# An encoder block on one core: branch A's queries and keys stored by map and loaded over 128 partitions, two gate products moved into branch A's stage

## The chip, the cores and the metric

The kernel runs on one core of a Trainium2 chip. The metric is the device time of one execution in microseconds, lower is better. A core has TensorE (PE, matmuls), VectorE (DVE), ScalarE (ACT), GpSimd (POOL) and SyncE (SP). SP issues every transfer of this kernel on one queue, in order; a transfer that has to wait holds all that are behind it in the queue. Sixteen DMA engines carry the transfers. SBUF, the on-chip memory, has 128 partitions; a tile is partitions x elements.

## What is computed

One encoder layer on 1024 tokens and 16 meta tokens of width 1024 in float32. Two attention branches run in parallel from the same normed input, are merged by two sigmoid gates, and a SwiGLU block follows:

```python
proj = rms_norm(h) @ w_in
# qa, ka: 4 heads x 2 maps x 64;  va: 4 heads x 128;  qb, kb, vb: branch B;  ga, gb: 1024 each
attn = softmax(q1 k1 / 8 + bias) - lam * softmax(q2 k2 / 8 + bias)     # branch A, per head
y_a  = rms_norm(attn @ va) * (1 - lambda_init)
y_b  = windowed attention with sinks (window 128, 8 heads on 2 key heads)
merged = sigmoid(ga) * (y_a @ w_ba) + sigmoid(gb) * (y_b @ w_bb)
h = h + merged @ w_o
h = h + (silu(h' @ w_gate) * (h' @ w_up)) @ w_down                     # h' = rms_norm(h)
out = rms_norm(h)[:, N_META:]
```

## The kernel before

**Numbers as pairs.** Each float32 operand of a matmul is split into a high part (ScalarE, a rounded copy) and a low part (the difference, by VectorE or GpSimd). A product is then three matmuls: high x high, high x low, low x high. `hT_hi` and `hT_lo` hold the normed, transposed input; the function `quad(hl, kh, half)` names a quarter of one of them (four of the eight row blocks, 512 of the tokens).

**Queries and keys of branch A.** `project_a(h)` projects head h: the queries in two chunks of 512 tokens, the values, and the keys in three chunks (384, 384, 272). Each chunk is copied out of PSUM into a stage tile (tag `qk`, three buffers, `QK_BUFS`), high part beside low part, and stored to DRAM by `q_consume` (L543) or `k_consume` (L546). The 128 partitions of a stage tile are map m = 0 or 1 times 64 elements. In DRAM, `qa_d[h]` and `ka_d[h]` are laid out [high or low, 128, tokens], so one store from all 128 partitions writes a chunk.

The score matmuls want it the other way round: for one map, partitions 0 to 63 hold the high part and 64 to 127 the low part, with a second copy of the keys in which the halves are swapped (`ks[m][:, 1]`). Two matmuls, one with each copy, then sum the products of high and low parts. `load_q` (L650) brings one map's queries with two transfers of 64 partitions, `load_k` (L654) its keys with four. `load_a1(h)` loads map 1 of head h, `load_a0(h)` map 0 and the values. The tiles have one buffer, so a transfer waits until the head before has made its last scores on that tile. `load_a1(0)` and the keys of map 0 of head 0 are asked for early, among the projections.

**Gate projections.** They are computed by a scheme with seven products per block of 256 gate columns in place of eight. A product (p, k) has number p and block k = 0 to 7; it is 12 matmuls, run in four steps of three. Products 5, 6, 7 and 3 use sums of weights, made by GpSimd (`weight_sums`) and kept in `ws_d`; products 5, 6, 7 and 4 use sums of token blocks, kept in `ts_d` and loaded over a quarter of `hT` by `load_sums` (L575) once that quarter is no longer read: number 5 over quarter (0, 1), and second, number 6 over quarter (1, 0). Product 2 needs no sums of either kind and reads quarter (1, 0). Before branch A starts, a loop (L711 to L722, matmuls at L718) runs product 2 for all eight k. All others are in `order_g` (L579): first (5, k) and (3, k), then (1, k), (6, k), (7, k), (4, k). `gate_steps` (L729, matmuls at L738) is a generator that yields after each step of `order_g`, and `g_ahead` (L636) asks for the weights (`g_load`, L620) four products ahead and splits them three ahead. The weights of the first two products are loaded and split before the stage, into tiles named `w_g` and `w_gop`.

**Branch A's stage.** Four heads of eight tiles of 128 queries. A tile makes scores for map 1, then map 0 (L797, three chunks of keys, two matmuls each), exponentials, the combination, transposes (L823), and the value matmuls (L836) of earlier tiles come in between. `SLOTS` mixes in one step of the gates at four places of a tile. `fill(n)` runs n steps at once: `G_HEAD` (10) at the start of heads 1 to 3, `G_FIRST` (0) at the start of head 0, `G_LAST` (4) after the last tile; `HOLD` (26) steps are kept for the end, where the last value matmuls leave room.

**What sets the order.** GpSimd's order is as written from the second half of the projections to the start of branch A, TensorE's is as written from branch A's stage on. Everything else (SP, VectorE, ScalarE, and TensorE in the projections) is ordered at build time by a planner, which simulates the program with its own costs for instructions and transfers and takes what is ready first, by order in the program where several are. So the queue of SP can hold a transfer ahead of one that the program names earlier. Memory of a closed pool is reused: the gate stage's weight tiles (`gpool`) lie where the weights and stage tiles of the projections were, and wait for the last reader of those.

Of the kernel before, what the change touches and what calls it, by code (L numbers as in the profile page):

```python
# [19 lines left out]
P = 128  # L20
# [23 lines left out]
GK_BUFS = 3  # L44
GR_BUFS = 5
GO_BUFS = 4
HOLD = 26
GT_BUFS = 4
WB_BUFS = 5
G_HEAD = 10  # L50
G_FIRST = 0
G_LAST = 4

QK_BUFS = 3
# [19 lines left out]
def encoder_block(ctx: ExitStack, tc: tile.TileContext, x, meta, norm_mix, w_in, lq1, lk1, lq2, lk2,  # L74
                  subln, sink, w_ba, w_bb, w_o, norm_ffn, w_g, w_u, w_d, norm_final, out, dbg=None):
    nc = tc.nc
# [5 lines left out]
    def f32(ap):  # L82
        return ap.bitcast(F32)
# [16 lines left out]
    qa_d = [dram.tile([2, P, S], F32, name=f"qa_d{h}") for h in range(AH)]  # L100
    ka_d = [dram.tile([2, P, L], F32, name=f"ka_d{h}") for h in range(AH)]
# [58 lines left out]
    def pp_bank(name):  # L160
        return bank(psum1, "pp", name, 3 if psum1 is not psum2 else PP2)
# [28 lines left out]
    order = [C_KB, C_QB, C_VB]  # L190
# [3 lines left out]
            on_vector = len(order)  # L194
            order += [C_QB + 2 * P, C_QB + 3 * P]
    on_vector = order[on_vector:] + [C_QB, (0, 1), (2, 3)]
    order += [(k, k + 1) for k in range(0, 8, 2)]
    prepped = {}

    def ensure(n):  # L200
# [19 lines left out]
    def project(col, chunks, name, evac):  # L220
        ensure(1)
        for i, _ in enumerate(project_steps(col, chunks, name, evac)):
            if i % DC == V_AT and turning_v:
                next(turning_v[0], None)
        ensure(W_BUFS - 1)

    def evac_split(scale, consume):
        def run(ps, at, n):
            st = stage.tile([P, 2, 512], F32R, tag="qk", name="qk_stage", bufs=QK_BUFS)
            hi, lo = st[:, 0, :n], st[:, 1, :n]  # L230
            if scale is None:
                nc.scalar.activation(hi, ps, AF.Copy)
                nc.vector.tensor_tensor(lo, ps, f32(hi), ALU.subtract)
            else:
                nc.scalar.activation(hi, ps, AF.Copy, scale=scale)
                nc.vector.scalar_tensor_tensor(lo, ps, scale, f32(hi), ALU.mult, ALU.subtract)
            consume(f32(st), at, n)
        return run
# [19 lines left out]
    def flush_v():  # L258
        for g in turning_v:
            for _ in g:  # L260
                pass
# [243 lines left out]
    def quad(hl, kh, half):  # L505
        return (hT_hi, hT_lo)[hl][:, 4 * kh:4 * kh + 4, half * 512:half * 512 + 512]
# [34 lines left out]

    def project_a(h):
        def q_consume(st, at, n):  # L543
            nc.sync.dma_start(qa_d[h][:, :, at:at + n].rearrange("a p t -> p a t"), st[:, :, :n])

        def k_consume(st, at, n):  # L546
            nc.sync.dma_start(ka_d[h][:, :, at:at + n].rearrange("a p t -> p a t"), st[:, :, :n])

        def va_evac(pt, k0, nb, kp):
            vs = stage.tile([P, 2, 4, P], F32R, tag="qk", name="va_stage", bufs=QK_BUFS)  # L550
            hi, lo = vs[:kp, 0, :nb, :], vs[:kp, 1, :nb, :]
            nc.scalar.activation(hi, pt, AF.Copy)
            nc.vector.tensor_tensor(lo, pt, f32(hi), ALU.subtract)
            nc.sync.dma_start(va_d[h][:kp, :, k0:k0 + nb, :], f32(vs)[:kp, :, :nb, :])

        project(C_QA + h * P, Q_CHUNKS, f"qa{h}", evac_split(-(2.0 ** (2 * h - 1)), q_consume))
        project_v(C_VA + h * P, f"va{h}", va_evac)
        project(C_KA + h * P, K_CHUNKS if h < AH - 1 else K_CHUNKS[::-1], f"ka{h}", evac_split(None, k_consume))
# [15 lines left out]
        for hl in range(2):  # L574
            nc.sync.dma_start(f32(quad(hl, kh, half)), ts_d[p][:, hl])  # L575

    G_ACT = {5: (0, 1), 3: (1, 1), 1: (0, 0), 6: (1, 0), 7: (0, 1), 4: (1, 1)}
    G_OUT = {2: (0, 0), 5: (1, 1), 3: (0, 1), 1: (0, 0), 6: (0, 1), 7: (1, 1), 4: (1, 0)}
    order_g = []  # L579
    for k in range(0, 8, 2):  # L580
        order_g += [(p, k + i) for p in (5, 3) for i in range(2)]
    for k in range(0, 8, 2):
# [3 lines left out]
    def g_weights(k, kh, c0, cn):  # L586
        at = (C_GB, C_GA)[k // 4] + k % 4 * 256 + c0
        return w_in[kh * 512:kh * 512 + 512, at:at + cn].rearrange("(c p) n -> p c n", p=P)
# [26 lines left out]
    def g_load(n, raw=None):  # L615
        p, k = order_g[n]
        if raw is None:
            raw = gpool.tile([P, 512], F32, tag="gr", name=f"gr{p}_{k}", bufs=GR_BUFS)
        raw = raw.rearrange("p (c n) -> p c n", n=P)
        nc.sync.dma_start(raw, ws_d[k][:, (5, 6, 7, 3).index(p)] if p in (5, 6, 7, 3) else  # L620
                          g_weights(k, *{1: (0, 0), 4: (1, P)}[p], P))
        g_raw[p, k] = raw

    def g_split(n, op=None):
# [22 lines left out]
    project_a(1)  # L647
    token_sums(3)

    def load_q(h, m, q):  # L650
        for hl in range(2):
            nc.sync.dma_start(f32(q)[64 * hl:64 * hl + 64], qa_d[h][hl, 64 * m:64 * m + 64, :])

    def load_k(h, m, k):  # L654
        for hl in range(2):
            for var in range(2):
                at = 64 * (hl ^ var)
                nc.sync.dma_start(f32(k)[at:at + 64, var, :], ka_d[h][hl, 64 * m:64 * m + 64, :])

    def load_a1(h):  # L660
        q = [None, vtpool.tile([P, S], F32R, tag="q1", name=f"aq{h}_1", bufs=1)]
        k = [lowpool.tile([P, 2, L], F32R, tag=f"k{m}", name=f"ak{h}_{m}", bufs=1) for m in range(2)]
        load_q(h, 1, q[1])
        load_k(h, 1, k[1])
        return q, k

    def load_a0(h, q, k):
        q[0] = apool.tile([P, S], F32R, tag="q0", name=f"aq{h}_0")
        load_q(h, 0, q[0])
        if h:  # L670
            load_k(h, 0, k[0])
        v = apool.tile([P, 2, 9, P], F32R, tag="v", name=f"av{h}")
        nc.gpsimd.memset(f32(v)[:, 0, 8, :], 0.0)
        nc.sync.dma_start(f32(v)[:, :, 0:8, :], va_d[h][:, :, 0:8, :])
        nc.sync.dma_start(f32(v)[:2 * NM, 0, 8, :], va_d[h][:2 * NM, 0, 8, :])
        nc.sync.dma_start(f32(v)[2 * NM:3 * NM, 0, 8, :], va_d[h][:NM, 1, 8, :])
        return q, k, v
# [30 lines left out]
        u0 = 896 - t * P  # L708
        nc.gpsimd.tensor_copy(dist_m[:, t, 0:S - last_k0], dist[:, u0 + last_k0:u0 + S])
    flush_v()  # L710
    for k in range(0, 8, 2):  # L711
        ensure(1)
        wh, wl = prepped.pop((k, k + 1))
        for i in range(2):
            ps = pp_bank(f"pg2_{k + i}")
            for c in range(4):
                for j, (a, b) in enumerate(((wh, 0), (wh, 1), (wl, 0))):
                    nc.tensor.matmul(ps, a[:, 4 * i + c], quad(b, 1, 0)[:, c], start=(c == 0 and j == 0), stop=(c == 3 and j == 2))  # L718
            st = f32(stage.tile([P, 2, 512], F32R, tag="qk", name="gate_first", bufs=QK_BUFS))[:, 0]
            nc.scalar.copy(st, ps)  # L720
            nc.sync.dma_start(g_place(2, k + i), st)
        ensure(W_BUFS - 1)  # L722
# [6 lines left out]
    def gate_steps():  # L729
        for n, (p, k) in enumerate(order_g):  # L730
            g_ahead(n + 1)
            op, act = g_ready.pop((p, k)), G_ACT[p]
            if p in (5, 1):
                g_bank[k] = pp_bank(f"pg{p}_{k}")
            ps = g_bank[k]
            for c in range(4):
                for i, (a, b) in enumerate(((0, 0), (0, 1), (1, 0))):
                    nc.tensor.matmul(ps, op[:, a, c], quad(b, *act)[:, c], start=(p in (5, 1) and c == 0 and i == 0),  # L738
                                     stop=(p in (3, 4) and c == 3 and i == 2), skip_group_check=True)
                if c == 3:  # L740
                    if p in (1, 6, 7):
                        st = g_kept.pop((p, k))
                        nc.vector.tensor_tensor(st, ps, st, ALU.add)
                    else:
                        st = gpool.tile([P, 512], F32, tag="g", name="gate_stage", bufs=G_BUFS)
                        nc.scalar.copy(st, ps)
                    nc.sync.dma_start(g_place(p, k), st)
                    if (p, k) in ((5, 3), (5, 7), (3, 7)):
                        later_p = {(5, 3): 6, (5, 7): 7, (3, 7): 4}[p, k]
                        load_sums(later_p, *G_ACT[later_p])  # L750
                yield
# [109 lines left out]

    n_gates = [4 * len(order_g) - HOLD]

# [28 lines left out]
    for n in range(AH * NT + T_LAG):  # L892
        scoring, turning = iter(()), iter(())
        if n < AH * NT:
            h, t = divmod(n, NT)
            if t == 0:
                if h:
                    ld = load_a0(h, *load_a1(h))
                fill(G_HEAD if h else G_FIRST)
            if t % 2 == 0:  # L900
# [26 lines left out]
        if n >= T_LAG and tiles[n - T_LAG][1] % 2:  # L927
            tail.append(later(tiles[n - T_LAG]))
    n_gates[0] += HOLD
    raw_w = []  # L930
# [28 lines left out]
    def ps_bank(name):  # L959
        return bank(psum3, "bank", name, 8)  # L960
# [57 lines left out]
    for o in range(DC):  # L1018
        w = first_w[o] if o < 2 else branch_w(ypool, o, w_bb, "b")
        for half in range(2):  # L1020
            gt, ps, tk = gated(0, o, half, w, yb)
# [16 lines left out]
    for n, (o, half) in enumerate(order_a):  # L1038
        if o not in ws_a:
            ws_a[o] = branch_w(ypool, o, w_ba, "a")  # L1040
        gt, ps, tk = gated(1, o, half, ws_a[o], ya)
# [211 lines left out]
    for t in range(4, NT):  # L1253
        ps = ps_bank(f"po_1_{t}")
# [27 lines left out]
    st = {}  # L1282
# [161 lines left out]
    for n in range(nf, len(steps)):  # L1444
        p, j = steps[n][1]
# [3 lines left out]
        if p in LOADS:  # L1449
            at, half, col = LOADS[p]  # L1450
            if at <= j < at + 4:
                t, cols = 4 * half + j - at, slice(col * 512, col * 512 + 512)
# [60 lines left out]
```

## Time and profile before

| | us |
|---|---|
| median of three runs | 1458.92 (1453.92 to 1460.4) |
| the profiled execution | 1456.24 |
| its span, first to last instruction | 1454.5 |
| TensorE busy | 1424.5 (98%) |
| branch A's stage, about | 331 to 633 |
| the loop of product 2, about | 305 to 331 |

The profile is of one execution. A row of the timeline is: start in us, duration in us, engine, line of the kernel, instruction, output <- inputs, partitions x elements, count, and in brackets the idle time of the engine before it with what ended that. A row of waits is: who waited for whom, total us, number of times, longest. A row of a window is: stretch, its length, then for PE, PEld (weight loads of TensorE), DVE, ACT and POOL the busy us and the number of instructions, then the granted clock of TensorE (1.00 is full), the mean busy share of the 16 DMA engines, and GB/s. A row of transfers is: output <- input, count, KB each, and the median us from issue to landing. A row of the chain is: start, us, what; it follows the work that ended last back from the end.

### The profile page before, as it was taken

What the parts mean: (1) busy time and instruction counts of PE and PEld (TensorE: products, weight loads), DVE (VectorE), ACT (ScalarE), POOL (GpSimd) and SP (SyncE); (2) the same over time, 40 slices, a digit from 0 to 9 for tenths busy, and PEclk for the clock granted to TensorE, in tenths of its full rate; (3) what the DMA queues carried; (4) which work ended last, traced back from release to release, by engine and by line L of the source; (5) the groups of instructions that cost most, each with busy time, mean ns of one, the idle gap of its engine ahead of it and who ended that gap; (6) DMA issues with size and microseconds to landing.
All of it is one profiled execution on the core that took longest, in us unless ns stands there. A gap on an engine that the chain in (4) does not pass through costs nothing.

```text
span 1454.5 us, 21164 instructions
## 1 busy us (share of the span) xinstructions
PE 1424.5 (98%) x7279; PEld 1219.8 (84%) x7279; DVE 896.9 (62%) x1624; ACT 681.2 (47%) x1289; POOL 644.9 (44%) x604
## 2 busy tenths in 40 slices
PE   8999999999999999999999999999999999999997
PEld 6998989988888889888888878888888888888886
DVE  7468536527687879743713876555555554777567
ACT  6366436545564555554412743333333333444454
POOL 4599127653333333333722665544545542000444
PEclk9999999999999999999999999999999999999999
DMA  8467668886558464576521434332223332964343
GB/s 242 88 208 242 189 164 281 273 279 212 156 193 231 162 189 155 180 239 210 181 95 75 143 109 152 123 108 96 101 101 108 103 100 97 335 214 138 123 128 140
DMA packets 188827, 242.41 MB, mean 167 GB/s; under 512 B 18144, under 2 KB 115872, under 8 KB 188720
## 3 DMA queue, kind: packets, MB, share of 16 engines
q1 hardware_dynamic: 188720, 241.07, 52.2%
q8 instruction: 57, 0.93, 0.3%
q14 instruction: 50, 0.41, 0.1%
HBM read 157.45 MB, written 77.00 MB: 161 GB/s over the span
## 4 chain that ended last, share of the span: by engine, by line
PE 60%; issue 4%; DMA 4%; POOL 4%; DVE 2%; ACT 1%; SPq 1%; POOLq 0%; DVEq 0%; ACTq 0%
PE pg L1294 27%; PE pd L1388 9%; PE po L1071 6%; PE pg L738 6%; PE ppa L781 5%; PE aps L797 3%; POOL oa L118 3%; PE apy L836 3%; DMA ak<-ka_d 2%; PE apt L823 2%; DVE as L800 1%; POOL wop L118 1%; DMA g_d<-gk 1%; PE pg L718 1%; DVE as L811 0%
## 5 line engine op out<-in xcount | busy, mean ns | idle before, releaser
L118 POOL TENSOR_TENSOR wop<-wf,wop 128x512 fp32r<-128x512 f32 x128 | 174.8, 1371 | 162.3 <-ACT wop L117 149.8
L1294 PE MATMUL pg<-t,wop 128*128 128x512 f32 x1056 | 242.9, 389 | 0.2 <-POOL wop L118 0.2
L1294 PEld LDWEIGHTS pg<-t,wop 128*128 128x128 f32 x1056 | 198.2, 188 | 41.7 <-POOL wop L118 0.6
L1388 PE MATMUL pd<-ob,oa 128*128 128x512 f32 x924 | 209.9, 389 | 0.4 <-POOL oa L118 0.4
L1388 PEld LDWEIGHTS pd<-ob,oa 128*128 128x128 f32 x924 | 173.4, 188 | 36.8 <-POOL oa L118 0.8
L1294 PE MATMUL pg<-b,wop 128*128 128x512 f32 x792 | 184.0, 390 | 2.3 <-DVE c L1303 2.3
L1294 PEld LDWEIGHTS pg<-b,wop 128*128 128x128 f32 x792 | 148.3, 188 | 33.7 <-issue 2.4
L738 PE MATMUL pg<-hT_hi,gop 128*128 128x512 f32 x368 | 137.0, 396 | 0.8 <-POOL gop L118 0.8
L117 ACT ACTIVATE wop<-wf 128x512 fp32r<-128x512 f32 x128 | 80.3, 632 | 85.9 <-PE pg L1294 49.1
L118 POOL TENSOR_TENSOR oa<-ra,oa 128x512 fp32r<-128x512 f32 x33 | 44.0, 1335 | 170.1 <-ACT oa L117 168.6
L118 POOL TENSOR_TENSOR gop<-gr,gop 128x512 fp32r<-128x512 f32 x46 | 62.6, 1361 | 119.2 <-ACT gop L117 119.2
L117 ACT ACTIVATE oa<-ra 128x512 fp32r<-128x512 f32 x77 | 48.7, 632 | 106.5 <-PE pd L1388 47.4
L797 PE MATMUL aps<-ak,aq 128*128 128x392 f32 (+1 forms) x384 | 90.6, 330 | 7.6 <-DMA ak<-ka_d 6.2
L805 ACT ACTIVATE as<-as,amn 128x1040 f32<-128x1040 f32 x64 | 74.5, 1165 | 47.2 <-DVE amn L800 40.3
L797 PEld LDWEIGHTS aps<-ak,aq 128*128 128x128 f32 x384 | 69.8, 189 | 23.0 <-issue 6.8
L1071 PE MATMUL po<-woh,mT 128*128 128x512 f32 x384 | 88.0, 390 | 0.0
L1129 DVE TENSOR_TENSOR s<-wf,wf 128x512 f32<-128x512 f32 x22 | 17.7, 806 | 108.9 <-DMA wf<-in_w_ff_gate_dram 54.8
L1071 PEld LDWEIGHTS po<-woh,mT 128*128 128x128 f32 x384 | 71.9, 188 | 14.8
L343 POOL TENSOR_SCALAR bs<-bs,bdn 128x432 f32<-128x432 f32 (+1 forms) x64 | 41.5, 667 | 87.9 <-DVE bdn L341 74.9
L738 PEld LDWEIGHTS pg<-hT_hi,gop 128*128 128x128 f32 x368 | 69.2, 188 | 11.9 <-POOL gop L118 1.3
L738 PE MATMUL pg<-hT_lo,gop 128*128 128x512 f32 x184 | 72.7, 395 | 0.0
L808 POOL TENSOR_SCALAR as<-as,adn,neglam 128x1040 f32<-128x1040 f32 x32 | 39.0, 1218 | 62.7 <-DVE adn L806 49.3
(287 smaller groups left out, 3120.8 us busy)
## 6 DMA issues: line engine op xcount, KB each, us to landing
ra<-aop SPq DMA_DIRECT2D x77, 256.0 KB, 2.7
wf<-in_w_ff_gate_dram SPq DMA_DIRECT2D x24, 512.0 KB, 3.6
wf<-in_w_ff_up_dram SPq DMA_DIRECT2D x24, 512.0 KB, 3.7
aop<-as SPq DMA_DIRECT2D x44, 256.0 KB, 2.1
w_c<-in_w_in_dram SPq DMA_DIRECT2D x17, 512.0 KB, 5.5
aop<-c SPq DMA_DIRECT2D x33, 256.0 KB, 2.0
ak<-ka_d SPq DMA_DIRECT2D x32, 260.0 KB, 6.2
ts_d<-to SPq DMA_DIRECT2D x16, 512.0 KB, 3.6
```

The costliest lines, as they stand in the source:

```text
L117: nc.scalar.activation(hi, src, AF.Copy)
L118: lo_eng.tensor_tensor(lo, src, f32(hi), ALU.subtract)
L343: nc.gpsimd.tensor_scalar(st[:, r, :W], st[:, r, :W], dn[:, r:r + 1], 1.0, ALU.mult, ALU.mult)
L738: nc.tensor.matmul(ps, op[:, a, c], quad(b, *act)[:, c], start=(p in (5, 1) and c == 0 and i == 0), stop=(p in (3, 4) and c == 3 and i == ...
L781: nc.tensor.matmul(ps, w[:, a, j, :], src(j, b, tk), start=(j == 0 and n == 0), stop=(j == 3 and n == 2))
L797: nc.tensor.matmul(ps[:, :n], qs[m][:, t * P:(t + 1) * P], ks[m][:, vv, k0:k0 + n], start=(vv == 0), stop=(vv == 1))
L805: nc.scalar.activation(s[m][:, 0:L], s[m][:, 0:L], AF.Exp, bias=low, scale=-1.0, accum_out=dn[:, m:m + 1])
L808: (nc.gpsimd if t % 4 in COMBINE_POOL else nc.vector).tensor_scalar(s[1][:, 0:L], s[1][:, 0:L], dn[:, 1:2], neglam, ALU.mult, ALU.mult)
L836: nc.tensor.matmul(py[:, cols], v[:kp, a, k, :], at_[:kp, k, b, :], start=(k == 0 and j == 0), stop=(k == 8))
L1071: nc.tensor.matmul(ps, mT[:, c, a, t * P:(t + 1) * P], wos[q, c][:, b], start=(c == 0 and n == 0), stop=(c == DC - 1 and n == 2))
L1294: nc.tensor.matmul(ps, op[:, x, c, :], b[:, y, c, :], start=(p in (1, 2, 5) and c == 0 and n == 0), stop=(p in (4, 2, 3) and c == 3 and n ...
L1388: nc.tensor.matmul(ps[u], oa[:, a, u * P:(u + 1) * P], ob[:, b, :], start=(p in (1, 2, 5) and j == 0 and k == 0), stop=(p in (2, 3, 4) and ...
```

## The change

Three parts. First, `qa_d` and `ka_d` are now laid out by map: `qa_d[h][m]` is [high 64, low 64] x tokens. Each chunk is stored by two transfers, one for each map, from 64 partitions each. A map's queries are loaded by one transfer of 128 partitions, its keys by one of 128 partitions and two of 64 for the swapped copy. Second, product 2 of blocks 6 and 7 leaves the loop ahead of branch A and becomes the first two entries of `order_g`; its weights are now what is loaded into `w_g` and split into `w_gop`. `G_FIRST` becomes 4, so (2, 6) runs ahead of head 0's first scores, and `HOLD` becomes 30. Third, it follows from the second that the second token sums (number 6, over quarter (1, 0)) can only be loaded after (2, 7) has read that quarter.

```diff
-HOLD = 26
+HOLD = 30
...
-G_FIRST = 0
+G_FIRST = 4
...
-    order += [(k, k + 1) for k in range(0, 8, 2)]
+    order += [(k, k + 1) for k in range(0, 6, 2)]
...
         def q_consume(st, at, n):
-            nc.sync.dma_start(qa_d[h][:, :, at:at + n].rearrange("a p t -> p a t"), st[:, :, :n])
+            for m in range(2):
+                nc.sync.dma_start(qa_d[h][m, :, at:at + n].rearrange("(a d) t -> d a t", a=2),
+                                  st[64 * m:64 * m + 64, :, :n])
 
         def k_consume(st, at, n):
-            nc.sync.dma_start(ka_d[h][:, :, at:at + n].rearrange("a p t -> p a t"), st[:, :, :n])
+            for m in range(2):
+                nc.sync.dma_start(ka_d[h][m, :, at:at + n].rearrange("(a d) t -> d a t", a=2),
+                                  st[64 * m:64 * m + 64, :, :n])
...
-    G_ACT = {5: (0, 1), 3: (1, 1), 1: (0, 0), 6: (1, 0), 7: (0, 1), 4: (1, 1)}
+    G_ACT = {2: (1, 0), 5: (0, 1), 3: (1, 1), 1: (0, 0), 6: (1, 0), 7: (0, 1), 4: (1, 1)}
...
-    order_g = []
+    order_g = [(2, 6), (2, 7)]
...
-                          g_weights(k, *{1: (0, 0), 4: (1, P)}[p], P))
+                          g_weights(k, *{2: (1, 0), 1: (0, 0), 4: (1, P)}[p], P))
...
-    def load_q(h, m, q):
+    def load_k(h, m, k):
+        nc.sync.dma_start(f32(k)[:, 0, :], ka_d[h][m])
         for hl in range(2):
-            nc.sync.dma_start(f32(q)[64 * hl:64 * hl + 64], qa_d[h][hl, 64 * m:64 * m + 64, :])
-
-    def load_k(h, m, k):
-        for hl in range(2):
-            for var in range(2):
-                at = 64 * (hl ^ var)
-                nc.sync.dma_start(f32(k)[at:at + 64, var, :], ka_d[h][hl, 64 * m:64 * m + 64, :])
+            nc.sync.dma_start(f32(k)[64 - 64 * hl:128 - 64 * hl, 1, :], ka_d[h][m, 64 * hl:64 * hl + 64, :])
...
-        load_q(h, 1, q[1])
+        nc.sync.dma_start(f32(q[1]), qa_d[h][1])
...
-        load_q(h, 0, q[0])
+        nc.sync.dma_start(f32(q[0]), qa_d[h][0])
...
-    for k in range(0, 8, 2):
+    for k in range(0, 6, 2):
         ensure(1)
         wh, wl = prepped.pop((k, k + 1))
...
-            if p in (5, 1):
+            if p in (2, 5, 1):
                 g_bank[k] = pp_bank(f"pg{p}_{k}")
...
-                    nc.tensor.matmul(ps, op[:, a, c], quad(b, *act)[:, c], start=(p in (5, 1) and c == 0 and i == 0),
-                                     stop=(p in (3, 4) and c == 3 and i == 2), skip_group_check=True)
+                    nc.tensor.matmul(ps, op[:, a, c], quad(b, *act)[:, c], start=(p in (2, 5, 1) and c == 0 and i == 0),
+                                     stop=(p in (2, 3, 4) and c == 3 and i == 2), skip_group_check=True)
```

## The prediction

> **What bounds the kernel now.** I read the page's totals first, then the chain, the waits of TensorE from 290 to 660 us, TensorE's rows at each wait, and last the DMA rates in short windows.
>
> ```profile
> span 1454.5 us, 21164 instructions
> PE 1424.5 (98%) x7279; PEld 1219.8 (84%) x7279; DVE 896.9 (62%) x1624; ACT 681.2 (47%) x1289; POOL 644.9 (44%) x604
> ...
> 73.00:240.00 167.00, 166.41 (x947) 150.69 (x948) 100.90 (x211) 88.10 (x200) 100.75 (x112) 1.00 0.68 207
> 240.00:331.00 91.00, 89.55 (x508) 79.48 (x507) 42.74 (x93) 45.28 (x96) 55.45 (x83) 1.00 0.87 280
> 331.00:633.00 302.00, 291.30 (x1746) 259.61 (x1745) 233.43 (x656) 170.97 (x320) 111.84 (x91) 0.99 0.59 182
> ...
> PE aps L797 <- DMA ak<-ka_d: 6.2, 6, 1.6
> PE apt L823 <- DVE as L811: 1.7, 2, 1.0
> PE pg L718 <- ACT gate_first L720: 1.5, 2, 0.8
> ```
>
> TensorE is the bound: 30 us of the span hold no matmul. Of these 10.7 lie in branch A's stage (331 to 633 us) and 1.5 in the stage ahead of it. The change can only win such gaps, since it adds and removes no matmul. The biggest group is the wait for the keys, six gaps, two at each of heads 1 to 3. Those of heads 2 and 3, with what they wait for:
>
> ```profile
> 468.87 0.40 PE L738 MATMUL pg<-hT_hi,gop 128*128 128x512 f32 x1
> 470.21 0.41 PE L797 MATMUL aps<-ak,aq 128*128 128x392 f32 x1 [0.94 <-DMA ak<-ka_d]
> 471.37 0.42 PE L797 MATMUL aps<-ak,aq 128*128 128x392 f32 x1 [0.75 <-DMA ak<-ka_d]
> ...
> 541.62 0.40 PE L738 MATMUL pg<-hT_hi,gop 128*128 128x512 f32 x1
> 543.58 0.42 PE L797 MATMUL aps<-ak,aq 128*128 128x392 f32 x1 [1.56 <-DMA ak<-ka_d]
> ...
> 529.04 6.21 DMA ak<-ka_d
> 535.27 9.38 DMA ak<-ka_d
> ...
> 472.00:476.00 4.00, 4.00 (x21) 3.86 (x20) 1.09 (x4) 1.23 (x2) 1.27 (x1) 0.57 1.04 393
> ```
>
> The 9.38 us is issue to landing of head 3's last key transfer: it ends at 544.65, and the matmul of 544.79 follows. By start times a gap is longer than the bracket says. Streaming matmuls of 512 columns start 0.23 us apart, so 468.87 to 470.21 loses 1.11 us, not 0.94, and 470.21 to 471.37 loses 0.96 instead of 0.75. That is 0.2 a gap, 1.2 on six: the waits cost 7.4 us. After head 2's gaps TensorE had a granted clock of 0.57 for 4 us, which is 4 x 0.43 = 1.7 us more.
>
> **The loads.** Are the keys late by distance or by rate? The rate decides, and the next rows price it: a weight load over 128 partitions, queries over two 64-partition halves, a store from 64 partitions, a store from 128, and the stretch of head 2's keys.
>
> ```profile
> 183.00:184.00 1.00, 1.00 (x6) 0.78 (x6) 0.00 (x0) 0.51 (x1) 0.00 (x0) 1.00 1.17 392
> 184.50:187.50 3.00, 3.00 (x15) 2.43 (x14) 0.47 (x1) 0.00 (x0) 0.00 (x0) 1.00 0.96 234
> 111.00:111.50 0.50, 0.50 (x5) 0.49 (x4) 0.50 (x2) 0.50 (x2) 0.50 (x1) 1.00 0.57 133
> 112.00:112.50 0.50, 0.50 (x4) 0.46 (x3) 0.50 (x2) 0.33 (x1) 0.50 (x1) 1.00 1.00 389
> 462.00:464.00 2.00, 2.00 (x10) 1.64 (x9) 1.56 (x3) 0.63 (x1) 0.81 (x1) 1.00 0.99 215
> ...
> ak<-ka_d SPq DMA_DIRECT2D x32, 260.0 KB, 6.2
> aq<-qa_d SPq DMA_DIRECT2D x16, 256.0 KB, 5.3
> ```
>
> With the 16 engines equally busy (last but one column), whole partitions move 390 GB/s and halves 215 to 234. I take 380 and 234. A map of one head is two query transfers (0.524 MB) and four key transfers (1.065 MB): 1.589/0.234 = 6.8 us. After the change queries and the first copy of the keys are whole (1.056/0.38 = 2.8 us) and the swapped copy stays in halves (0.532/0.234 = 2.3): 5.1 us. Two maps come 3.5 us earlier. Head 3's last keys land at about 541.2 while TensorE gets there at 541.85. Head 2's would land at 467.7 against 469.1. All six gaps close, by margins of 0.7 to 1.4 us. SP issues 8 transfers in place of 12 at a head, so the values, gate weights and stores behind them also start some 2 us sooner. What is late next is the vector work on scores:
>
> ```profile
> 478.09 0.62 PE L797 MATMUL aps<-ak,aq 128*128 128x392 f32 x2 [0.57 <-DVE amn L800]
> ```
>
> VectorE caught up while TensorE stood; I leave 0.5 us a head for it: 7.4 + 1.7 - 1.5 = 7.6 us gained. Ends: 9.1, and 3 if most of the gaps only change their releaser.
>
> The clock is where a rule and a row differ. The rows show 0.57 straight after gaps of about 1 us each, and at one head of three. The Trainium skill, in TensorE: Matmul & The Clock Gate, "The HAM clock gate", has the clock halve only after a whole idle window of about 3.4 us; no gap here is that long, so the trace does not agree. By the page the 1.7 us is not owed to these gaps and may stay: 5.9 gained in place of 7.6.
>
> **The stores.** A query chunk goes out as two transfers from 64 partitions, a key chunk too: 20 more issues on SP over four heads, 16 fewer for loads. The row at 111 us is a 64-partition store: 133/0.57 = 233 GB/s for a busy engine, against 389 a moment later. Queries and keys are 8.45 MB: 36.1 us of engine time for 21.7, so 14.4 more. The loads for head 0 in the same stretch save 2.7. Cover: the engines idle for 32% of 167 us and 13% of 91 us. In the tight second stretch heads 2 and 3 add 5.1 us there, while a weight load and two gate stores leave it with 1 MB (2.8 us) and head 0's queries save 0.5: under 2 us net on 12 idle. So it stays beside TensorE, but for one place where buffers are short:
>
> ```profile
> 308.13 0.49 ACT L232 ACTIVATE qk_stage<-pp_ka 128x384 fp32r<-128x384 f32 x1 [1.60 <-DMA va_d<-va_stage]
> 311.12 0.59 ACT L720 COPY gate_first<-pg 128x512 f32<-128x512 f32 x1 [2.50 <-DMA ka_d<-qk_stage]
> 319.11 0.50 PE L718 MATMUL pg<-hT_hi,wh_c 128*128 128x512 f32 x1 [0.75 <-ACT gate_first L720]
> 320.54 0.50 PE L718 MATMUL pg<-hT_hi,wh_c 128*128 128x512 f32 x1 [0.70 <-ACT gate_first L720]
> ```
>
> ScalarE waited for a stage buffer that a key store still held, and TensorE for ScalarE. That store (0.393 MB) takes 1.7 us of engines in place of 1.0: I charge 0.6 us. Ends: 1.5 gained (the gaps go with the two products), 14.4 lost (no cover at all).
>
> **The moved products.** Two of eight products without sums, (2,6) and (2,7), leave the gate loop: 24 matmuls at 10.50/44 = 0.239 us are 5.7 us less before branch A and 5.7 more in it.
>
> ```profile
> 320.54 10.50 PE pg L718 x44
> ...
> 330.83 0.37 SPq L575 DMA_DIRECT2D hT_lo<-ts_d  x1
> 331.30 0.46 SPq L575 DMA_DIRECT2D hT_hi<-ts_d  x1
> 331.85 0.46 SPq L721 DMA_DIRECT2D g_d<-gate_first  x1
> 332.41 8.13 SPq L620 DMA_DIRECT2D gr<-ws_d  x3
> ...
> 343.49 0.51 PE L738 MATMUL pg<-hT_hi,gop 128*128 128x512 f32 x1 [0.84 <-POOL gop L118]
> 348.61 1.51 PE L823 MATMUL apt<-ident,as 128*128 128x128 f32 x9 [0.99 <-DVE as L811]
> ```
>
> TensorE is full on both sides, so that is zero. Copies out of PSUM, splits and stores move with them one for one, and their weight splits take the place of others that follow in branch A, where GpSimd is busy 112 of 302 us. Four of the eight steps run before the first scores, four are held for the end, where TensorE is full and they only delay the next stage by what the loop got shorter: zero too.
>
> What changes is the order on SP. Now the second token sums (two transfers of 1 MB, L575) are asked for at 330.83, ahead of the gate weights; the last gate store behind them lands late, the second and third weights go out near 340, and TensorE waits 0.84 for a split and 0.99 and 0.2 for a chain that the same burst delays: 2.0 us. With (2,6) and (2,7) still reading that quarter, the sums can only follow them and the weights go first. The rows that price the first of these weights, for (5,0):
>
> ```profile
> gr<-ws_d SPq DMA_DIRECT2D x30, 256.0 KB, 3.4
> 340.44 0.63 ACT L117 ACTIVATE gop<-gr 128x512 fp32r<-128x512 f32 x1
> L118 POOL TENSOR_TENSOR gop<-gr,gop 128x512 fp32r<-128x512 f32 x46 | 62.6, 1361 | 119.2 <-ACT gop L117 119.2
> 330.88 0.52 PE L797 MATMUL aps<-ak,aq 128*128 128x392 f32 x2
> 331.24 0.40 PE L738 MATMUL pg<-hT_hi,w_gop 128*128 128x512 f32 x1
> ```
>
> It takes 3.4 + 0.6 + 1.4 = 5.4 us plus issue and hand-overs, after the last gate matmul has freed its place. It is wanted after four steps (2.8) and tile 0 (four steps, 2.8, and six score pairs, 0.36 or a little less each, 1.9): 7.5 us. That is enough with 1 or 2 us in hand, if nothing else is in the queue. I take half the waits, 1.0 gained; ends 2.0 gained and, if SP kept the sums ahead, 8 lost.
>
> **The sum.** -7.6 + 0.6 + 0 - 1.0 = -8.0 us. The profiled execution took 1456.24 (span 1454.5), so 1448.2 on its terms. The median of the runs shown, 1458.92, is 2.7 above it: 1450.9.
>
> **Rivals.**
> - The next-late work takes the gaps. VectorE is busy 233 of 302 us in branch A and already released gaps there; against it, each of those is under 1.1 us. Gain 3 to 5: about 1455.
> - The change does not do what it says: the swapped copy still comes in halves, last, and the second matmul of each pair waits for it. Those second gaps are about 1.0 us each by starts; with the clock loss kept, 4.7 of 9.1 stay: gain 4.4 + 0.4 (the other terms) = 4.8, 1454.1. Against it stands the 3.5 us computed above.
> - The first gate weights come late. If SP holds the sums, waiting for (2,7), in front of the weights, everything behind SP stands until tile 0 ends; then 2 MB (2.1/0.38 = 5.5 us) and a weight's path (5.4) follow: TensorE stands some 10 us, of which 2 are there today. -7.0 + 8 = +1: 1460. What speaks against it: the program asks for the weights first, and the sums are free later than now.
> - The other side: the half-rate stores reach TensorE. Place: the key phases, where three stage buffers carry six evacuations. The wait of 2.50 us speaks for it, the idle engines against it. It decides from 8.6 us on, the gain of the other terms; at the full 14.4 the time is 1458.9 - 8.6 + 14.4 = 1464.7. The Trainium skill, in SBUF — State Buffer, "Can I just issue two DMAs to hit both halves?", says two transfers to the two halves do not add up to a whole one, and its table has 196 GB/s for 64 partitions against 328 for 128. The 233 and 389 above agree in ratio. By the page's figures the extra would be 8.45/0.196 - 8.45/0.328 = 17 us, an estimate.
>
> **How the numbers follow.** About 0.5% (7.3 us) is what a measurement of this kernel tells from no change. Forecast 0.54 (its own range 1446 to 1455), vector work 0.10, second copies 0.10, late weights 0.11, stores 0.15. Faster by over 0.5% means below 1451.6: most of the forecast's half, 0.50. Slower by over 0.5% means above 1466.2: only the stores with a reordered queue on top, 0.10. The rest, 0.40, is within. Low end: all gaps named (9.1 + 2.0 + 1.5 = 12.6) with runs 4 us below the median: 1442. High end: between late weights and the stores' full price, 1463.
>
> **What would show it.** Right: no wait for ak at heads 1 to 3, clock 1.00 there, key transfers of 520 KB, the gate loop some 5.7 us shorter, gate weights ahead of the second L575 pair. Wrong: gaps at L797 released by ak or VectorE, a gap at the first step of (5,0), longer waits for qk_stage between 73 and 325 us, or a planner's new order of SP, VectorE and ScalarE in that stretch, which no row of before can price.

## The result and the profile after

| | us |
|---|---|
| before, median (five runs beside the changed kernel) | 1458.92 (1453.92 to 1460.56) |
| changed, median of five runs | 1447.57 (1445.82 to 1449.07) |
| ratio, with its 95% interval | 0.9926 [0.9904, 0.9949] |
| the profiled execution, changed | 1446.1, span 1444.3 |

The change wins 11.4 us here, 0.7% by the ratio. Two later measurements are told below: 0.9966 [0.9952, 0.9979] and 0.9959 [0.9946, 0.9972], 4.8 and 5.3 us. The first interval and the second do not overlap. In those sessions the kernel before ran in 1455 us and the changed one in 1450, so the gain is 5 to 11 us, and one session's interval is narrower than what lies between sessions.

The page's totals, windows (columns as in the prediction; the second, third and fourth stretch are cut anew) and TensorE's waits from 290 to 660 us of the changed kernel, whose line numbers behind the gate functions are one lower (the gate steps are L737, the scores L796):

```profile
span 1444.3 us, 21160 instructions
PE 1422.8 (99%) x7279; PEld 1221.2 (85%) x7279; DVE 899.2 (62%) x1624; ACT 679.6 (47%) x1290; POOL 641.3 (44%) x605
...
73.00:240.00 167.00, 166.81 (x951) 151.08 (x951) 101.23 (x213) 88.20 (x201) 101.14 (x113) 1.00 0.70 207
240.00:323.00 83.00, 83.00 (x480) 74.68 (x479) 42.16 (x91) 42.62 (x92) 52.90 (x81) 1.00 0.92 288
323.00:380.00 57.00, 54.42 (x313) 48.74 (x312) 42.97 (x136) 35.77 (x68) 22.20 (x18) 0.97 0.50 172
380.00:633.00 253.00, 251.14 (x1506) 224.11 (x1505) 193.97 (x528) 145.93 (x271) 93.18 (x77) 1.00 0.61 200
...
PE apt L822 <- DVE as L810: 2.6, 2, 1.9
PE aps L796 <- DVE amn L799: 0.6, 1, 0.6
...
```

The same three new stretches of the kernel before:

```profile
240.00:323.00 83.00, 81.55 (x474) 73.01 (x473) 42.74 (x93) 43.52 (x93) 53.48 (x82) 1.00 0.90 288
323.00:380.00 57.00, 54.74 (x316) 48.28 (x315) 40.07 (x124) 33.63 (x64) 21.39 (x17) 1.00 0.50 176
380.00:633.00 253.00, 244.56 (x1466) 217.81 (x1466) 193.36 (x532) 139.10 (x260) 92.42 (x77) 0.99 0.61 184
```

Length minus TensorE's busy time is its idle time:

| idle, us | 73–240 | 240–323 | 323–380 | 380–633 | sum |
|---|---|---|---|---|---|
| before | 0.6 | 1.5 | 2.3 | 8.4 | 12.7 |
| changed | 0.2 | 0.0 | 2.6 | 1.9 | 4.6 |

The wait for the keys (6.2 us, six times) is gone from the list, and the stretch that held it has 6.6 us less idle. Two later profiles of the changed kernel are not quite as clean: from 380 to 633 us they have 3.0 and 3.9 us idle, and the third has one wait for keys again:

```profile
PE aps L796 <- DMA ak<-ka_d: 0.7, 1, 0.7
```

Over the whole span idle falls by 8.5 (30.0 to 21.5) and busy by 1.7, which is the span's 10.2 us. Part of the 1.7 is the 0.2 us a gap of the prediction: a matmul is drawn 0.40 us long, and where they stream the next one starts 0.23 after it. How the rest divides is not shown.

Two things are new. The first is at tile 0 of head 0. The next fence has the profile's timeline of VectorE, ScalarE, SP and TensorE there, and three windows:

```profile
328.70 0.08 DVE L799 DVE_READ_ACCUMULATOR2_ANT amn<- 128x1 f32 x1
...
328.13 0.63 ACT L117 ACTIVATE gop<-gr 128x512 fp32r<-128x512 f32 x1 [1.62 <-DMA gr<-ws_d]
330.63 0.63 ACT L117 ACTIVATE gop<-gr 128x512 fp32r<-128x512 f32 x1 [1.86 <-DMA gr<-ws_d]
332.10 1.15 ACT L804 ACTIVATE as<-as,amn 128x1040 f32<-128x1040 f32 x1
...
325.01 2.79 SPq L624 DMA_DIRECT2D gr<-ws_d  x4
330.67 0.37 SPq L579 DMA_DIRECT2D hT_lo<-ts_d  x1
...
338.03 1.64 PE L822 MATMUL apt<-ident,as 128*128 128x128 f32 x9 [1.94 <-DVE as L810]
...
337.00:338.50 1.50, 0.47 (x4) 0.47 (x5) 1.50 (x4) 1.50 (x4) 0.00 (x0) 1.00 1.06 411
338.50:341.50 3.00, 3.00 (x13) 2.62 (x12) 2.85 (x11) 2.58 (x6) 2.46 (x2) 0.53 1.05 404
341.50:343.00 1.50, 1.50 (x8) 1.36 (x7) 1.15 (x7) 0.00 (x0) 0.00 (x0) 0.81 1.07 400
```

The gate weights go out at 325.01, ahead of the second token sums (L579), as the prediction said. But ScalarE had splits ahead of the exponentials in its order: VectorE had the maxima (`amn`) of tile 0's first map at 328.78, while ScalarE stood 1.86 us for weights it was to split and reached the first exponential only at 332.10. The chain behind it (combination, transposes) is late, TensorE stands 1.94 us, and the granted clock is 0.53 and 0.81 for the next 4.5 us: 3.0 x 0.47 + 1.5 x 0.19 = 1.7 us. The kernel before lost as much behind head 2's gaps.

The second is how the keys come. SP's issues at head 1, and the first issue and last issues of head 3 with the score matmuls of map 0 there (chain, start, us, what), of the changed kernel:

```profile
378.54 0.32 SPq L662 DMA_DIRECT2D aq<-qa_d  x1
378.91 0.42 SPq L655 DMA_DIRECT2D ak<-ka_d  x1
379.39 1.14 SPq L657 DMA_DIRECT2D ak<-ka_d  x2
380.89 0.33 SPq L668 DMA_DIRECT2D aq<-qa_d  x1
381.26 0.43 SPq L655 DMA_DIRECT2D ak<-ka_d  x1
...
382.22 1.10 SPq L657 DMA_DIRECT2D ak<-ka_d  x2
...
515.11 0.32 SPq L662 DMA_DIRECT2D aq<-qa_d  x1
...
519.49 0.66 SPq L657 DMA_DIRECT2D ak<-ka_d  x1
...
DMA to landing us min/median/max: 9.3/9.4/9.8
...
531.14 0.35 PE aps L796 x2
```

and head 1 of the kernel before:

```profile
382.46 1.09 SPq L652 DMA_DIRECT2D aq<-qa_d  x2
383.61 1.86 SPq L658 DMA_DIRECT2D ak<-ka_d  x3
...
388.06 1.10 SPq L652 DMA_DIRECT2D aq<-qa_d  x2
389.79 2.99 SPq L658 DMA_DIRECT2D ak<-ka_d  x4
```

From the first issue to the end of the last, a head's loads took 10.3 us before (382.46 to 392.78) and take 4.8 now (378.54 to 383.32). The last key transfers of head 3 are issued by 519.49 and land some 9.4 later, the last at about 529; the first scores of map 0 start at 531.14 without a wait. From first issue to last landing head 3 took 18.7 us before (525.98 to 544.65) and takes about 14. The 4.8 us hold one gate store too, the 10.3 a gate store and a store of `yg`.

### The profile page after: what moved, and what is told of

It reads as the page before. It is cut to its first block, busy times and chain, and to the rows that moved or that the text cites. A ratio compares the mean times of both kernels' runs of the same rounds, so it can differ in the third digit from the quotient of the medians.

```text
span 1444.3 us, 21160 instructions
## 1 busy us (share of the span) xinstructions
PE 1422.8 (99%) x7279; PEld 1221.2 (85%) x7279; DVE 899.2 (62%) x1624; ACT 679.6 (47%) x1290; POOL 641.3 (44%) x605
## 4 chain that ended last, share of the span: by engine, by line
PE 81%; POOL 6%; DVE 5%; issue 4%; DMA 2%; ACT 1%; POOLq 0%; SPq 0%; DVEq 0%; ACTq 0%
PE pg L1293 28%; PE pd L1387 9%; PE pg L737 7%; PE po L1070 6%; PE ppa L780 6%; PE aps L796 3%; PE pp_qb L214 3%; POOL oa L118 3%; PE apy L835 3%; PE pp_ka L214 2%; PE pp_va L214 2%; PE apt L822 2%; PE pp_qa L214 2%; PE bpt L356 1%; PE bpy L362 1%
## 5 line engine op out<-in xcount | busy, mean ns | idle before, releaser
L737 PE MATMUL pg<-hT_hi,gop 128*128 128x512 f32 x384 | 142.7, 396 | 0.0
L1128 DVE TENSOR_TENSOR s<-wf,wf 128x512 f32<-128x512 f32 x22 | 25.0, 1138 | 108.1 <-DMA wf<-in_w_ff_gate_dram 58.0
L796 PE MATMUL aps<-ak,aq 128*128 128x392 f32 (+1 forms) x384 | 90.0, 330 | 1.3 <-DVE amn L799 0.6
L796 PEld LDWEIGHTS aps<-ak,aq 128*128 128x128 f32 x384 | 69.6, 189 | 15.0 <-DVE amn L799 2.2
L737 PEld LDWEIGHTS pg<-hT_hi,gop 128*128 128x128 f32 x384 | 72.7, 189 | 11.2 <-DVE gk L742 0.2
L737 PE MATMUL pg<-hT_lo,gop 128*128 128x512 f32 x192 | 76.0, 396 | 0.0
```

What stands on the lines that cost most here:

```text
L796: nc.tensor.matmul(ps[:, :n], qs[m][:, t * P:(t + 1) * P], ks[m][:, vv, k0:k0 + n], start=(vv == 0), stop=(vv == 1))
```

## The experiments

Theory: the keys come earlier because of whole partitions, and that is the whole gain; the stores hide. Rivals: the gate part carries some of it, the stores eat some, or it is the number of transfers and not their shape.

### Layout alone, and gates alone

The kernel before with the new stores and loads, but with the gates as they were:

```diff
 HOLD = 26
 G_FIRST = 0
-nc.sync.dma_start(qa_d[h][:, :, at:at + n].rearrange("a p t -> p a t"), st[:, :, :n])
+for m in range(2):
+    nc.sync.dma_start(qa_d[h][m, :, at:at + n].rearrange("(a d) t -> d a t", a=2),
+                      st[64 * m:64 * m + 64, :, :n])
...
+nc.sync.dma_start(f32(q[1]), qa_d[h][1])
```

> The stores in halves and the loads over whole partitions alone; the gate products stay where they were. If the rate of the loads is what was won, the waits for ak at heads 1 to 3 are gone and the kernel is 8 to 9 us below the one before (ratio about 0.994), with the gap of some 2 us at the start of branch A still there. If the moved gate products carry the gain, it is within 3 us of the kernel before (above 0.998).

Measured: 1447.84 us, the kernel before beside it 1455.71, ratio 0.9943 [0.9928, 0.9957]. None of its waits is for keys.

The other half: the moved products, `G_FIRST` 4 and `HOLD` 30, with the old stores and loads.

```diff
-HOLD = 26
+HOLD = 30
-G_FIRST = 0
+G_FIRST = 4
...
-    order_g = []
+    order_g = [(2, 6), (2, 7)]
```

> The two moved products with 4 steps ahead and 30 held, with queries and keys stored and loaded as before. If the rate of the loads is the cause: six waits for ak, about 6 us, remain, and the kernel is 0 to 3 us below the one before (ratio 0.998 to 1.000). If the products carry the gain: 8 us or more below (0.9945 or less).

Measured: 1456.13 us, ratio 1.0005 [0.9995, 1.0014]. TensorE's waits (290 to 660 us) and a window of it:

```profile
PE aps L797 <- DMA g_d<-gk: 3.0, 1, 3.0
PE aps L797 <- DMA ak<-ka_d: 2.6, 3, 1.9
...
330.00:345.00 15.00, 11.60 (x48) 9.57 (x47) 8.86 (x30) 9.44 (x18) 8.70 (x7) 0.77 0.99 354
```

The layout alone has the gain, 7.9 us; the gate part alone has none, between 0.7 us faster and 2.0 slower. Its waits for the keys stay: 2.6 us by name, and the 3.0 us stand at the same line at 468.67, at head 2's keys, where the profile names a store as the last to come. New idle time with a clock of 0.77 stands at the start of the stage.

The layout alone was run again beside the changed kernel, on one chip:

> The layout alone on the chip of the changed kernel. If the moved products and the earlier weights are worth the 1.0 us that was forecast, it is 0 to 2 us slower than the changed kernel of this call; if the new gap at tile 0 of head 0 eats what they bring, within 1 us either way; if that gap and its clock loss cost more than they bring, 1 to 3 us faster.

> The changed kernel, beside the three others of this call: the two measurements of it so far gave 0.9926 and 0.9966 of the kernel before. If both are draws of one spread, this one lies between them, 0.993 to 0.997.

Measured: layout alone 1448.04 us, 0.9945 [0.9932, 0.9958]; the changed kernel 1449.81, 0.9959 [0.9946, 0.9972]. The layout alone is 1.8 us less, with intervals that overlap. Its windows:

```profile
240.00:323.00 83.00, 81.08 (x470) 72.76 (x469) 41.38 (x91) 42.58 (x92) 53.45 (x81) 1.00 0.93 290
323.00:380.00 57.00, 55.74 (x322) 49.35 (x321) 41.59 (x129) 35.42 (x67) 22.46 (x19) 1.00 0.48 171
380.00:633.00 253.00, 250.44 (x1506) 224.16 (x1504) 196.53 (x536) 145.52 (x270) 92.26 (x76) 1.00 0.60 198
```

Idle 1.9, 1.3 and 2.6 us. Against it the changed kernel saves the 1.9 us ahead of the stage, since the last two products left that loop, and pays them back at tile 0 (from 323 to 380 us 2.6 in its first profile and 3.4 in the two later ones instead of 1.3, and in two of the three the clock). The gate part trades one gap for another; that it costs anything on the whole is not shown.

The changed kernel was also timed a second time beside the runs on columns and on the start of the stage below:

> The changed kernel once more, beside the next three on the same chip: ratio to the kernel before 0.9925 to 0.9945. With the layout alone at 0.9943 and the gate products alone at 1.0005, a sum of the two would be 0.9948; a value under 0.993 would say that the products are worth more once the keys are early.

Measured: 1450.36 us, before 1455.20, ratio 0.9966 [0.9952, 0.9979], above what was expected. The third time, beside the layout alone, it lay within.

### The stores alone

```diff
-nc.sync.dma_start(ka_d[h][:, :, at:at + n].rearrange("a p t -> p a t"), st[:, :, :n])
+for m in range(2):
+    nc.sync.dma_start(ka_d[h][:, 64 * m:64 * m + 64, at:at + n].rearrange("a p t -> p a t"),
+                      st[64 * m:64 * m + 64, :, :n])
```

The kernel before with this for keys and queries: the data go to the old places, only from 64 partitions at a time.

> The kernel before with each query and key chunk stored by two transfers of 64 partitions, in the old places, and loaded as before. If the engines' idle time covers the slower stores, as the prediction has it, the time is 0 to 1 us above the kernel before (ratio 1.000 to 1.001), with the waits for ak as they were. If halves reach TensorE through the stage buffers, 3 to 14 us above (1.002 to 1.010).

Measured: 1456.95 us, ratio 1.0008 [0.9999, 1.0017], so 1.2 us more, at most 2.5.

```profile
240.00:323.00 83.00, 80.93 (x473) 72.85 (x472) 42.42 (x95) 44.19 (x96) 53.26 (x82) 1.00 0.92 287
...
PE pg L722 <- ACT gate_first L724: 2.1, 1, 2.1
```

Idle from 240 to 323 us is 2.1 in place of 1.5, all of it at the place that the prediction named. The layout-alone runs have 2.1 and 1.9 there too. Of the 14.4 us of extra engine time nearly all lies beside TensorE.

### The loads in halves, by columns, and with a small cut

The changed kernel with its loads in 64-partition halves again, from the new places:

```diff
-nc.sync.dma_start(f32(q[1]), qa_d[h][1])
+for hl in range(2):
+    nc.sync.dma_start(f32(q)[64 * hl:64 * hl + 64], qa_d[h][m, 64 * hl:64 * hl + 64, :])
...
+for hl in range(2):
+    for var in range(2):
+        at = 64 * (hl ^ var)
+        nc.sync.dma_start(f32(k)[at:at + 64, var, :], ka_d[h][m, 64 * hl:64 * hl + 64, :])
```

> The changed kernel, but with queries loaded in two transfers of 64 partitions and keys in four, from the new places: everything of the change but the whole loads. If the loads carry the gain: waits for ak of about 6 us at heads 1 to 3 again, and 8 to 10 us above the changed kernel (ratio to the kernel before 0.998 to 1.000). If the new order on SP or the gates do: within 3 us of the changed kernel (0.994).

Measured: 1457.18 us, ratio 1.0009 [0.9996, 1.0021]. The gain is gone and the wait is back, `ak` 3.9 us in five gaps, and 1.9 more at head 2's keys under a store's name. So the gain is in the loads. Next, the changed kernel with whole partitions, but queries and first key copy cut into two transfers by columns, so that a head has twelve again:

```diff
-nc.sync.dma_start(f32(q[1]), qa_d[h][1])
+for i in range(2):
+    nc.sync.dma_start(f32(q)[:, 512 * i:512 * i + 512], qa_d[h][m, :, 512 * i:512 * i + 512])
...
-nc.sync.dma_start(f32(k)[:, 0, :], ka_d[h][m])
+for i in range(2):
+    nc.sync.dma_start(f32(k)[:, 0, 520 * i:520 * i + 520], ka_d[h][m, :, 520 * i:520 * i + 520])
```

> The changed kernel with the queries and the first copy of the keys loaded over whole partitions, but in two transfers each, by columns: 12 transfers on SP at a head as in the kernel before, not 8, at the rate of whole partitions. If the rate is what was won, no wait for ak and within 2 us of the changed kernel (ratio 0.993 to 0.996). If the shorter queue on SP was (the values, gate weights and stores behind the keys start some 2 us sooner), 4 us or more of the gain is lost (above 0.996).

Measured: 1454.15 us, ratio 0.9990 [0.9981, 0.9999], 3.8 us above the changed kernel of the same session (1450.36), and the intervals do not overlap. Two lines of it:

```profile
323.00:380.00 57.00, 51.06 (x299) 44.80 (x298) 40.91 (x126) 33.73 (x64) 20.38 (x17) 1.00 0.48 175
...
PE aps L801 <- DMA ak<-ka_d: 1.9, 2, 1.3
```

Whole partitions alone keep only a part of the gain. Of the loss in the profiles (spans 1452.5 and 1446.0) some 2.6 us lie at tile 0 of head 0 (5.9 idle, 3.4 in the changed kernel of the session), where the first gate weights go out at 327.70 in place of 325.69, and some 2.7 at the heads (5.7 idle from 380 to 633 us in place of 3.0). Is that the number of transfers or the shorter rows (2 KB)? The cut was put at column 8: a transfer of 4 KB and one of nearly the whole size.

```diff
-nc.sync.dma_start(f32(q[1]), qa_d[h][1])
+for a, b in ((0, 8), (8, S)):
+    nc.sync.dma_start(f32(q)[:, a:b], qa_d[h][m, :, a:b])
```

> The changed kernel with the query load and the first key copy each cut by columns again, so twelve transfers a head as in the run with equal columns, but at column 8: a small transfer of 4 KB and one of nearly the whole size (rows of 4 KB). Theory one, the number of transfers on SP counts: the loss of the equal cut is still there, 3 to 5 us above the changed kernel of this call, and gaps of 0.5 to 1.5 us before tile 0 or at the keys of head 1. Theory two, the size of a transfer or the length of its rows counts: within 1.5 us of the changed kernel, rate at the heads as in it (317 to 384 GB/s).

Measured: 1453.08 us, ratio 0.9986 [0.9970, 1.0001]; the changed kernel of that session had 1449.81. SP's issues at head 1, what SP waited for from 376 to 396 us, and TensorE's wait for the keys, of this run:

```profile
381.40 0.80 SPq L656 DMA_DIRECT2D aq<-qa_d  x2
382.25 0.90 SPq L660 DMA_DIRECT2D ak<-ka_d  x2
383.19 1.14 SPq L662 DMA_DIRECT2D ak<-ka_d  x2
...
385.05 1.01 SPq L656 DMA_DIRECT2D aq<-qa_d  x2
...
386.64 2.56 SPq L660 DMA_DIRECT2D ak<-ka_d  x2
390.02 1.33 SPq L662 DMA_DIRECT2D ak<-ka_d  x2
...
SPq L660 <- DMA ak<-ka_d: 1.5, 1, 1.5
...
PE aps L801 <- DMA ak<-ka_d: 3.7, 2, 2.6
```

Twelve transfers take 10.0 us to issue (381.40 to 391.35) with long rows, 10.8 with short ones (381.85 to 392.65), and the twelve of the kernel before took 10.3; the first eight go out in 4.7 us, and then SP stands for keys of the same head that have yet to land. So eight in place of twelve counts: it carries 3.3 and 3.8 us of the changed kernel's gain in these two comparisons, and whole partitions the rest. The sizes have the uncertainty of the two intervals, which here just overlap; the order of issues is plain at each head (12.5 and 9.6 us at heads 2 and 3, against 5.3 and 5.0 in the changed kernel). TensorE stands for keys 1.2 and 2.6 us at heads 1 and 2 in this run, 1.3 and 0.6 in the run with equal columns, and not at head 3 in either: there whole partitions alone were in time. Both runs also have more rows, 640 a map in place of 384; the kernel before, with 384, was as slow to issue, but its bytes moved at half the rate. Why SP stands there, by transfers, by rows or by bytes in flight, no run tells apart.

The Trainium skill, in DMA: Bandwidth & Descriptors, "Rules for kernel authors", tells to use one transfer over 128 partitions in place of two over disjoint halves, since the two share the same engines. The run in halves agrees (ratio 1.0009, the changed kernel 0.9926 to 0.9966). Two transfers over all partitions, cut by columns, cost about half of that: 3.3 and 3.8 us, where the halves cost 6 to 7 by the two later ratios.

The other way, six transfers a head: the high part of the keys is stored a second time, so that the swapped copy is whole as well.

```diff
+nc.sync.dma_start(ka_d[h][m, P:P + 64, at:at + n], st[64 * m:64 * m + 64, 0, :n])
...
+for var in range(2):
+    nc.sync.dma_start(f32(k)[:, var, :], ka_d[h][m, 64 * var:64 * var + P, :])
```

> The changed kernel with the high part of the keys stored a second time, so that the swapped copy comes by one transfer of 128 partitions too: six transfers a head, all over whole partitions, and 24 more stores of 64 partitions (2.1 MB) ahead of branch A. If the keys of the changed kernel are in time (margin 0.7 to 1.4 us), loads that are faster still gain nothing: within 1.5 us of the changed kernel of this call. If late loads still set its pace, 2 to 4 us faster. If stores from 64 partitions reach TensorE, 2 to 9 us slower, with longer waits for stage buffers between 240 and 325 us.

Measured: 1447.35 us, ratio 0.9941 [0.9928, 0.9954], 2.5 us under the changed kernel of the session with overlapping intervals. One of its windows:

```profile
240.00:323.00 83.00, 79.89 (x465) 71.68 (x464) 42.06 (x91) 41.88 (x91) 52.21 (x81) 1.00 0.92 289
```

A head's loads are issued in 4.4 us, hardly less than 4.8, and the additional stores now do reach TensorE: 3.1 us idle ahead of the stage, 1.8 of it one wait for ScalarE's copies in the gate loop (321.24). But from 380 to 633 us 1.3 us are idle, where the changed kernel of the session has 3.9 (0.7 of it a wait for keys, most of the rest waits for VectorE). So that kernel's keys were not all in time; whether the faster loads win the rest is not shown. The profiled spans, 1445.7 and 1446.2, do not differ. Whether the 2.5 us are real stays open.

### The gap at tile 0

If the gap comes from weights that ScalarE waits for, more gate steps ahead of the first scores give them time. The changed kernel with eight instead of four, and then also with the third product's weights loaded early into a third buffer:

```diff
-HOLD = 30
+HOLD = 26
-G_FIRST = 4
+G_FIRST = 8
...
-    for n in range(2):
+    for n in range(3):
         g_load(n, tpool.tile([P, 512], F32, tag="ta", name=f"w_g{n}", bufs=3))
...
-    g_done[:] = [2, 2]
+    g_done[:] = [3, 2]
```

> The changed kernel with 8 steps ahead of the first scores and 26 held: both products without sums run before tile 0. The changed kernel stands 0.64 and 1.94 us in its first tiles and then runs at half clock for some 3 us, while ScalarE waits for the gate weights ahead of the first exponentials. If the weights' lateness is the cause, 2.8 us more of TensorE work in front of it takes away most of that: 2 to 4 us below the changed kernel (ratio 0.990 to 0.993). If the planner merely puts ScalarE's splits ahead of the exponentials, whenever the weights come, the gap stays: within 1 us of the changed kernel.

> As the one with 8 steps ahead, and the raw weights of the third product, (5, 0), are asked for before the stage, into the third free buffer beside those of the first two. If late weights are the cause, its first tiles have no gap that a gate split ends, and it is 0 to 1 us below the kernel with 8 steps; if ScalarE's order is, the same as that one.

Measured: 1447.15 us, 0.9944 [0.9931, 0.9956], and 1446.48, 0.9947 [0.9934, 0.9959], where the changed kernel of the session had 1450.36. Window 323 to 380 us of the first and of the second:

```profile
323.00:380.00 57.00, 55.01 (x318) 48.51 (x318) 40.92 (x129) 35.76 (x68) 22.89 (x19) 1.00 0.52 187
```

```profile
323.00:380.00 57.00, 53.45 (x310) 47.08 (x308) 40.16 (x124) 34.19 (x65) 20.99 (x17) 1.00 0.51 183
```

The idle time there is 2.0 and 3.5 us: the one gap of 1.95 is replaced by smaller ones, and the clock is at 1.00. With eight steps two of them end with a gate split (0.83 and 0.67 us); with the third product's weights loaded early none does, as the theory of late weights expected. The medians are 3 to 4 us lower, yet the intervals overlap a little and the profiled spans (1446.4 and 1445.1, against 1446.0) do not show it. These two, the run with six loads and the layout alone are all 0.994 to 0.995: none is shown to beat the changed kernel, whose own three ratios surround them.

## Why the prediction was right or wrong

Forecast: 1450.9, range 1442 to 1463, faster by over 0.5% with 0.50. Measured: 1447.57, and 1450.36 and 1449.81 later. The forecast gain of 8.0 us lies between the three measured, 11.4, 4.8 and 5.3, of which only the first is over 0.5%. That the sum fits this well is in part luck: the 1.0 us of the order on SP did not come, and the price of the loads left out what the number of transfers does.

- **What bounds it.** Right. TensorE did the same matmuls, and only gaps moved: idle 30.0 to 21.5 us.
- **The keys, 7.6 us.** Right in size: from 380 to 633 us idle falls by 6.6 in the first profile of the changed kernel, by 5.5 and 4.6 in the later two, and the 1.7 us of clock behind head 2's gaps are gone in all three (1.00 against 0.99 in the window), 6.3 to 8.3 in all; the layout-alone runs gain 7.9 and 7.1 with the stores' cost in it. The charge of 0.5 us a head for VectorE, 1.5 in all, was too high: the waits there that VectorE ends took 2.2 us before and take 1.7, 2.8 and 3.0 in the three profiles.
- **"The rate decides".** This step failed in part. Two maps do come earlier, measured from the first issue, by somewhat more than the forecast 3.5 (head 3: 18.7 to about 14). But the bytes by 234 and 380 GB/s are not all that sets it: with the first copies whole and twelve transfers, 3.3 to 3.8 us of the gain were lost, in the first of the two profiles about half at the heads and half at tile 0. The prediction counted 8 issues in place of 12 only for what stands behind them in the queue, while they held back the keys themselves at heads 1 and 2, and the first gate weights. The rows of issues at head 1, shown above, were in the trace before and were not priced.
- **The stores, 0.6 us.** Right: 0.5 to 0.6 us idle more at the named place, 1.2 [-0.1, 2.5] in time. The rival's 14.4 us are engine time that TensorE hardly sees. So are the 17 us, the estimate by the Trainium skill (SBUF — State Buffer, "Door 1: The DMA port swizzle").
- **The moved products, nothing; the order on SP, 1.0 gained.** The order came as foretold, weights first. The gain did not: the gates alone measured 0.7 us slower [-0.7, +2.0]. The failing step is "with 1 or 2 us in hand". That sum priced when TensorE gets the weights of the first gate step. It left out that ScalarE splits weights and makes the exponentials in one order, so weights that are late for no matmul still delayed the scores: 1.94 us idle and, in two of three profiles, 1.7 us of clock. On the other side the end of the range for the stores, 1.5 us of loop gaps that go with the two products, did come (240 to 323 us without any idle time).
- **Rivals.** The second copies keep no waits but one, 0.70 us at head 2 in the third profile (at 464.26, the second matmul of a pair). Late first weights happened in a milder form, through ScalarE and not through SP. The work that is late next is VectorE's, but small.

## What to carry to other kernels

Where a wait is for loads, read the issuing queue before pricing bytes: the time from the first issue of the group to the last, and what the queue stood for in between; fewer transfers may be worth about as much as faster ones. Price a moved operand on every engine that handles it in order, not only on the one that consumes it. And time each part of a joint change alone: here one part carried everything and the other only moved a gap.

## What the runs showed of the hardware

The clock. The gap of 1.94 or 1.95 us at tile 0 stands in several of these kernels, and what follows differs. First the second run of the changed kernel, then its third:

```profile
341.00:344.00 3.00, 3.00 (x9) 2.46 (x8) 2.98 (x9) 1.07 (x2) 1.01 (x1) 0.50 1.06 400
```

```profile
338.32 1.20 PE L822 MATMUL apt<-ident,as 128*128 128x128 f32 x9 [1.94 <-DVE as L810]
...
337.00:344.00 7.00, 5.56 (x30) 4.79 (x31) 6.85 (x19) 4.37 (x9) 2.47 (x2) 1.00 1.05 403
```

In the second run the clock fell to half for 3 us, in the third it stayed full. The amount of idle time does not decide it: the second and third had 3.4 us idle each from 323 to 380 us, and the run with equal columns, with gaps of 2.12 and 1.95 us there, kept the full clock too. A gap of 2 us so costs 1.7 us more or nothing, for the same program. This is one source of the spread between runs: the twelve executions cut at column 8 go from 1449.09 us at a mean granted clock of 0.999 to 1460.10 at 0.993. The Trainium skill, in TensorE: Matmul & The Clock Gate, "The HAM clock gate", tells of a free-running window of 3413 ns, idle for the whole of which halves the clock. A free-running window fits a loss that comes and goes and lasts about 3 us; the need of a whole idle window does not fit, since no gap of these three runs is longer than 2.12 us.

The queue. Over all profiles eight transfers to a head went out in 4.8 to 6.0 us, with what SP issued in between; where there were twelve, the last ones waited for landings and it took 9.1 to 12.5 us, also where four of the twelve had 4 KB only. With eight SP stands as well, but behind the keys: at head 1 of the changed kernel two gate stores wait 2.5 us for keys to land, and TensorE does not wait for those.
